# Filling the first buffer of a row-sum kernel with three loads in place of two

## The chip, the cores and the metric

The kernel runs on one core of a Trainium2 chip. The metric is device time in microseconds (us), the median of several runs. The engines that matter here are SyncE (SP), which issues all transfers; VectorE (DVE) and ScalarE (ACT), which add; and the core's 16 DMA engines, which move the data.

## The reference

```python
def setup_inputs():
    batch, seq, dim = 32, 512, 1024
    return {"x": np.random.randn(batch, seq, dim).astype(np.float32)}

def reference(x):
    return np.sum(x, axis=-1).astype(np.float32)
```

The input holds 16,384 rows of 1,024 float32 numbers, 67.1 MB in all. Each row is summed to one number, so the output is 64 KB. Every number is read once and added once.

## The kernel before, in words

The rows are spread over the 128 partitions of on-chip memory, 128 rows each. They are cut into three blocks of 32, 48 and 48 rows per partition (`BLOCKS`, line 10). Within a block, a partition's rows lie behind one another in memory, so that a partition's share of a load is one contiguous run.

Three buffers `xt0` to `xt2` of 16 rows per partition (64 KB per partition, 8.389 MB in all) are filled in turn. Lines 80 to 87 list the groups: seven of 16 rows. The last 16 rows come in smaller pieces: 9, 4 and 2 rows into the buffer that is then due (`CUTS`, lines 97 and 98), and the very last row in two parts of 544 and 480 columns into `tail` (lines 99 to 101).

Lines 92 to 95 write down the loads of the seven groups. Each group is one load, except the first, which is split in two: row 0 of each partition, which counts on the semaphore `first`, and rows 1 to 15, which count on `slot0`. A landed load adds 16 to its semaphore.

DVE waits for `first` (line 106) and then, for each group, for the group's slot (line 109). It then sums the whole group by one reduce over 16 rows (`rows_dve`, line 56). The first group's reduce thus starts when both loads have landed; no instruction uses row 0 alone. In the last group ACT takes 7 of the 16 rows (`rows_act`, line 67), and it takes a part of the pieces behind it. DVE sums the last rows by adding two halves (`pairs_dve`, line 74).

SP issues the loads in the order of the list (lines 135 to 138). From the fourth group on it first waits until DVE has summed what lay in the buffer. After the loads come three early stores of results, and then the last store (line 147).

All of this lies behind an opening barrier of the engines. Lines 174 to 182 take the first `EARLY` loads out of the body and put them ahead of SP's drain in the entry block, so that SP issues them before the barrier. `EARLY` is 2 here: both loads of the first group.

Of the kernel before, what the change touches and what calls it, by code (L numbers as in the profile page):

```python
# [11 lines left out]
BUFS = 3  # L12
ACT_ROWS = 7
CUT = 544
CUTS = (0, 9, 13, 15)
EARLY = 2


def row_sums(nc, x: bass.AP, out: bass.AP):
    P = nc.NUM_PARTITIONS  # L20
    x_flat = x.flatten_outer_dims()
    R, D = x_flat.shape
# [4 lines left out]
    xs, outs = [], []  # L27
# [6 lines left out]
    def sbuf(name, n):  # L34
        return nc.alloc_sbuf_tensor(name, [P, n], F32)

    xt = [sbuf(f"xt{i}", G * D) for i in range(BUFS)]
# [9 lines left out]
    sems = {n: nc.alloc_semaphore(n) for n in names}  # L47
    slots = [sems[f"slot{i}"] for i in range(BUFS)]
# [32 lines left out]
    for k, n in enumerate(BLOCKS):  # L81
        c = 0
        end = n - G if k == len(BLOCKS) - 1 else n
        while c < end:
            m = min(G, end - c)
# [4 lines left out]
    freed = {}  # L90
    loads = []
    for b, (k, c, m) in enumerate(groups):
        parts = [(0, m, slots[b % BUFS])] if b else [(0, 1, sems["first"]), (1, m, slots[0])]
        for i, j, s in parts:
            loads.append((b, xt[b % BUFS][:, i * D : j * D], xs[k][:, (c + i) * D : (c + j) * D], s))
    last = xt[n_bufs % BUFS]
    for k, (i, j) in enumerate(zip(CUTS, CUTS[1:])):
        loads.append((n_bufs, last[:, i * D : j * D], x_z[:, (z0 + i) * D : (z0 + j) * D], sems[f"piece{k}"]))
# [4 lines left out]

    nc.vector.memset(tail[:, CUT + 15 : CUT + 16], 0.0).then_inc(vec, 1)  # L104
    count["vec"] += 1
    nc.vector.wait_ge(sems["first"], 16)
    for b, (k, c, m) in enumerate(groups):
        a = ACT_ROWS if b == n_bufs - 1 else 0
        nc.vector.wait_ge(slots[b % BUFS], 16 * (b // BUFS + 1))
# [7 lines left out]
    for k in range(2):  # L117
        i, j = CUTS[k], CUTS[k + 1]
# [36 lines left out]
def kernel(tc: tile.TileContext, x: bass.AP, out: bass.AP):  # L155
    tc.close()
    tc.compile()  # L157
    nc = tc.nc
    row_sums(nc, x, out)

    sp = mybir.EngineType.SP
    fn = nc.m.functions[0]
    entry, body = None, None
    for blk in fn.blocks:
        ops = [i for i in blk.instructions if i.engine == sp]
        if entry is None:
            entry = blk
        elif any(i.opcode == "DMACopy" for i in ops):  # L170
            body = blk
            break
    code = list(body.instructions)
    loads = [i for i in code if i.engine == sp and i.opcode == "DMACopy"][:EARLY]
    for load in loads:
        assert not load.sync_info.on_wait
        code.remove(load)
    body.instructions = code
    code = list(entry.instructions)
    at = next(k for k, i in enumerate(code) if i.engine == sp and i.opcode == "Drain")  # L180
    code[at:at] = loads
    entry.instructions = code
# [29 lines left out]
```

## Time and profile before

| what | value |
|---|---|
| median of 3 runs | 160.51 us (160.5 to 160.61) |
| the profiled execution's own time | 160.68 us |
| span of that execution, first to last instruction | 159.3 us |
| DVE busy | 121.4 us (76%) |
| ACT busy | 17.2 us (11%) |
| read from HBM | 67.11 MB, 422 GB/s over the span |
| first load (512 KB), issue to landing | 3.5 us |
| second load (7680 KB), issue to landing | 21.3 us |

Times inside an execution count from the start of its span, which here is SP's first issue. The span is shorter than the execution's time by what lies around it, 1.38 us here. In the tables of stretches a DMA packet's bytes and time are booked to the stretch in which it starts; where packets last longer than a stretch, a share of DMA can exceed 1. Besides the groups and stretches, the trace has a record of every DMA packet: its start, its duration and its size. A packet is one partition's contiguous run of one load.

### The profile page before, as it was taken

To read this page: it belongs to the slowest core of one execution; us is meant where nothing else is said; L and a number is where in the kernel's file an instruction comes from. 1 tells how busy PE (TensorE), PEld (TensorE's weight loads), DVE (VectorE), ACT (ScalarE), POOL (GpSimd) and SP (SyncE) were. 2 spreads that over 40 slices of the span, in tenths; PEclk is the share of its full clock that TensorE was granted. 3 is DMA by queue.
4 is the path that set the end of the run, shared out by engine and by line. 5 is a ranking of instruction groups with operands and counts; after the bars stand their busy time and mean duration, and the time that the engine had idled before them with its cause. 6 is when DMAs were issued, how large, how long until landed. Compare 5 with 4: busy or idle time off the path is not lost.

```text
span 159.3 us, 109 instructions
## 1 busy us (share of the span) xinstructions
DVE 121.4 (76%) x16; ACT 17.2 (11%) x31; POOL 0.2 (0%) x4
## 2 busy tenths in 40 slices
DVE  0000059998699968999599994999949999499785
ACT  3000000000000000000000000000000000394694
POOL 0000000000000000000000000000000000000000
DMA  9988996996996999979969969969969989699994
GB/s 378 494 386 355 494 526 263 526 510 280 526 494 296 526 395 395 526 329 461 526 280 510 526 263 526 510 280 526 494 296 526 428 362 526 296 444 444 391 409 138
DMA packets 2448, 67.18 MB, mean 422 GB/s; under 512 B 784, under 2 KB 912, under 8 KB 1168
## 3 DMA queue, kind: packets, MB, share of 16 engines
q1 hardware_dynamic: 2448, 67.18, 98.1%
HBM read 67.11 MB, written 0.07 MB: 422 GB/s over the span
## 4 chain that ended last, share of the span: by engine, by line
DMA 75%; DVE 22%; SPq 1%; issue 0%
DMA xt<-in_x_dram 50%; DMA tail<-in_x_dram 25%; DVE res L56 22%; SPq L138 1%; DVE pairs L74 0%; DVE res L74 0%
## 5 line engine op out<-in xcount | busy, mean ns | idle before, releaser
L56 DVE TENSOR_REDUCE res<-xt 128x16 f32<-128x16384 f32 (+3 forms) x9 | 119.8, 13309 | 34.1 <-DMA xt<-in_x_dram 34.1
L67 ACT ACTIVATE xt<-xt 128x1024 f32<-128x1024 f32 x15 | 15.6, 1042 | 138.2 <-DMA xt<-in_x_dram 138.2
L67 ACT ACTIVATION_READ_ACCUMULATOR xt<-xt 128x1 f32 x15 | 2.8, 186 | 0.0
L104 DVE MEMSET tail<- 128x1 f32 x1 | 0.1, 59 | 2.0 <-PEq L157 2.0
L67 ACT ACT_TABLE_LOAD x1 | 1.3, 1283 | 1.9 <-PEq L157 1.9
L74 DVE CUSTOM_DVE_ANT_0 pairs<-tail 128x272 f32<-128x272 f32 (+1 forms) x2 | 0.9, 427 | 0.2 <-DMA tail<-in_x_dram 0.2
L74 DVE CUSTOM_DVE_ANT_0 pairs<-xt 128x512 f32<-128x512 f32 x1 | 0.7, 692 | 0.2 <-DMA xt<-in_x_dram 0.2
L74 DVE DVE_READ_ACCUMULATOR2_ANT res<- 128x1 f32 x2 | 0.2, 82 | 0.0
L196 POOL MEMSET const-bfloat16-1.0<- 128x1 bf16 x1 | 0.1, 102 | 0.0
L196 POOL MEMSET const-uint8-127<- 128x1 uint8 x1 | 0.1, 102 | 0.0
L196 POOL MEMSET const-float32-1.0<- 128x1 f32 x1 | 0.1, 99 | 0.0
L196 POOL MEMSET const-float32-0.0<- 128x1 f32 x1 | 0.1, 98 | 0.2 <-issue 0.2
L74 DVE DVE_READ_ACCUMULATOR2_ANT tail<- 128x1 f32 x1 | 0.1, 83 | 0.0
## 6 DMA issues: line engine op xcount, KB each, us to landing
xt<-in_x_dram SPq DMA_DIRECT2D x1, 7680.0 KB, 21.3
xt<-in_x_dram SPq DMA_DIRECT2D x1, 4608.0 KB, 32.4
xt<-in_x_dram SPq DMA_DIRECT2D x1, 2048.0 KB, 36.9
xt<-in_x_dram SPq DMA_DIRECT2D x1, 1024.0 KB, 38.9
xt<-in_x_dram SPq DMA_DIRECT2D x1, 512.0 KB, 3.5
tail<-in_x_dram SPq DMA_DIRECT2D x1, 272.0 KB, 39.1
tail<-in_x_dram SPq DMA_DIRECT2D x1, 240.0 KB, 39.2
xt<-in_x_dram SPq DMA_DIRECT2D x6, 40.8
```

The lines of the kernel that those rows point to most:

```text
L56: nc.vector.tensor_reduce(out=res[:, c : c + n], in_=t[:, j * D : (j + n) * D].rearrange("p (j d) -> p j d", d=D), axis=X, op=ADD,).then_i ...
L67: nc.scalar.activation(out=v, in_=v, func=COPY, accum_out=res[:, c + i : c + i + 1]).then_inc(act, 1)
L74: nc.vector.tensor_tensor_reduce(out=pairs[:, 0 : h - a], in0=t[:, a:h], in1=t[:, h:b], scale=1.0, scalar=0.0, op0=ADD, op1=ADD, accum_out ...
L104: nc.vector.memset(tail[:, CUT + 15 : CUT + 16], 0.0).then_inc(vec, 1)
L138: nc.sync.dma_start(out=dst, in_=src).then_inc(s, 16)
L196: nc = _bacc.Bacc("TRN2", target_bir_lowering=False, num_devices=1)
```

## The change

The first group is loaded by three loads: columns 0 to 511 of row 0, then the next 1,024 columns (the second half of row 0 and the first half of row 1), then the other 14.5 rows. The first two count on `first`, for which DVE now waits until 32; the third counts on `slot0`. `EARLY` becomes 3, so that all three are issued ahead of the barrier. The loads of the other groups are the same; their bounds are now written in columns.

```diff
-EARLY = 2
+EARLY = 3
+LEADS = (0, 512, 1536)
...
     for b, (k, c, m) in enumerate(groups):
-        parts = [(0, m, slots[b % BUFS])] if b else [(0, 1, sems["first"]), (1, m, slots[0])]
+        parts = [(0, m * D, slots[b % BUFS])]
+        if b == 0:
+            parts = [(i, j, sems["first"]) for i, j in zip(LEADS, LEADS[1:])] + [(LEADS[-1], m * D, slots[0])]
         for i, j, s in parts:
-            loads.append((b, xt[b % BUFS][:, i * D : j * D], xs[k][:, (c + i) * D : (c + j) * D], s))
+            loads.append((b, xt[b % BUFS][:, i:j], xs[k][:, c * D + i : c * D + j], s))
...
-    nc.vector.wait_ge(sems["first"], 16)
+    nc.vector.wait_ge(sems["first"], 32)
```

## The prediction

> **What bounds the kernel now.** I read the page from the top: the busy row of DMA, the share of the one queue, the chain of work that ended last.
>
> ```profile
> span 159.3 us, 109 instructions
> ...
> DMA  9988996996996999979969969969969989699994
> ...
> q1 hardware_dynamic: 2448, 67.18, 98.1%
> ...
> DMA 75%; DVE 22%; SPq 1%; issue 0%
> ```
>
> The reader is to see that the packets fill 98.1% of sixteen DMA engines' span. The chain's 22% of DVE is no second bound, as the groups and the waits show: DVE is released by a landing before every one of its reduces.
>
> ```profile
> L56 DVE TENSOR_REDUCE res<-xt 128x16 f32<-128x16384 f32 x6 | 103.3, 17220 | 30.4 <-DMA xt<-in_x_dram 30.4
> ...
> L56 DVE TENSOR_REDUCE res<-xt 128x4 f32<-128x4096 f32 x1 | 4.4, 4420 | 1.2 <-DMA xt<-in_x_dram 1.2
> ...
> L56 DVE TENSOR_REDUCE res<-xt 128x2 f32<-128x2048 f32 x1 | 2.3, 2285 | 0.5 <-DMA xt<-in_x_dram 0.5
> ```
>
> The timeline of DVE gives the pace: reduces of a full buffer start at 21.83, 41.10, 60.47, 79.82, 99.16 and 118.52 us, every 19.35 us or so, while one takes 17.22. A buffer is 8.389 MB, so the stream runs at 8.389 MB / 19.35 us = 434 GB/s. DVE waits 0.2 us for the last row pair and 0.2 us for the last tail piece too. Every wait on the way is ended by a landing, so **a shift of the whole DMA stream goes through to the end one for one**, in both directions.
>
> The change touches only the start of that stream. So the view that matters is the table of stretches at the start:
>
> ```profile
> core 0: us, DVE busy (x) ACT busy (x) POOL busy (x), PEclk, DMA share, GB/s
> 0.00:1.00 1.00, 0.00 (x0) 0.00 (x0) 0.20 (x4) 1.00 0.00 0
> 1.00:1.50 0.50, 0.00 (x0) 0.00 (x0) 0.00 (x0) 1.00 1.19 262
> 1.50:2.00 0.50, 0.02 (x1) 0.09 (x1) 0.00 (x0) 1.00 0.86 279
> ...
> 6.00:20.00 14.00, 0.00 (x0) 0.00 (x0) 0.00 (x0) 1.00 0.97 421
> ```
>
> Nothing moves in the first microsecond: the first load is issued at 0.00 and its first packet starts at 1.00 us. In the second microsecond the engines are occupied (a packet is booked where it starts, hence shares over 1) but move 262 and 279 GB/s instead of 434. That is a loss of about 0.38 us (1 - 270/434). The records of single DMA packets in the trace say where: the first load is 128 packets of 4,096 B, eight on each engine. The sixteen first ones start between 1.00 and 1.28 us. 89 of the 128 take under 170 ns (159 is typical) and 39 take up to 740, all of these started before 2.4 us. Per engine they sum to 1.65 us; eight at 157 ns, the usual pitch, would be 1.26. So **the start costs 0.40 us**, and the packets of the second load (61,440 B, typically 2,267 ns) another 0.11 us over that norm; two that started before 3 us exceed it by 268 and 327 ns. No engine stands idle between the two loads: added up, 15 to 16.5 engines are busy in every tenth of a microsecond from 1.2 us on.
>
> **The change part by part.** The same bytes come in the same order; one 4,096 B packet per partition becomes two, 2,048 and 4,096 B, and the long one shrinks from 61,440 to 59,392 B.
>
> *One more load.* 128 more packets and 16 more semaphore writes, so 8 and 1 on each engine. What a cut costs, from other packets of the trace: 8,192 B takes 309 ns and two of 4,096 B take 318, so 9 ns; 1,920 and 2,176 B together, again 4,096 B, take 79 + 88 = 167 against 159, so 8 ns. Eight cuts at 8.5 ns are 68 ns; a semaphore write is 9 ns. That makes **+0.08 us**.
>
> *Its issue.* SP's first two issues take 373 and 424 ns, at 0.00 and 0.42 us; a third, from about 0.9 us, takes some 0.43 (issues in a row take 437 to 462). While later loads were issued, at 58.35, 77.71 and 97.07 us, packets then in flight took about 15 ns longer. I put down **+0.01 us**.
>
> *What is moved.* The third load goes in ahead of SP's drain, so the opening barrier comes 0.45 us later, at about 2.35 instead of 1.9. Behind it stand SP's next issue (the load of buffer 1, at 1.91 now), ScalarE's table load and DVE's memset. The engines reach buffer 1 at 20.7 us, ACT's first row comes at 137.9, the zero is used at 157.4: all are covered by 17 us or more, and I put nothing down. If the cover were gone it would be 0.45 us. SP's later issues wait for DVE (112.3 us in five waits), so nothing is late there. POOL issues no load.
>
> *The wait.* DVE's first wait asks for 32 instead of 16: two loads landed rather than one. The first lands 3.5 us after issue now; the two will have landed by about 4 to 5 us. Behind it DVE has only the wait for the rest of the buffer, which ended at 21.8 us. It costs nothing, up to 17 us of delay.
>
> *Is the next load ready?* This trace doesn't show a first load so short. Each engine has eight packets of 2,048 B, about 80 ns each (1,920 B take 79 and 2,176 take 88): 0.65 us. An engine that loses nothing starts at 1.00 and would be through at 1.65. The second load is issued 0.42 us behind the first. Lags from issue to first packet with idle engines are 1.00 us (first load), 0.84 us (first store, 156.16 to 157.00) and 0.93 us (second store, 156.55 to 157.48). So its packets are due at 1.26 to 1.42 us, 0.2 us ahead of need. The third is due at about 1.9, and the second ends at 2.9 or later. I put down nothing; a lag over 1.22 us would show as idle engines.
>
> *The slow start.* What it becomes with shorter packets isn't in this trace, and I bound it from both sides. If slowness belongs to the first microsecond, whatever is asked for, it stays: 0. If it belongs to bytes in the first round of packets, half as many bytes could take as little as half of it, or all of 0.51 us might go. If it belongs to packets (39 of 128 slow), there are sixteen short ones per engine where there were eight, and another 0.40 us is lost. By time of start the mean is 327 ns up to 1.3 us, 243 to 1.6, 196 to 2.0, 166 to 2.4 and 159 after: it fades with time, while packet size is the same throughout. That is nearest to the first reading, so I take 0 and keep -0.51 and +0.40.
>
> **A rule against the change.** The last two loads, of 272 and 240 KB, run from full engines at 88 and 79 ns a packet (2,176 B / 88 ns x 16 = 395 GB/s): size alone hardly hurts a load that has others around it. The Trainium skill, page "DMA: Bandwidth & Descriptors", section "Bandwidth", tells authors to batch to 1 MiB or more, and its measured table has 64 KB in 0.95 us and 1 MB in 6.15 us. A line through these leaves about 0.6 us that every load would pay, an estimate from that page; by it the added load would make the kernel 0.6 us slower, while by the rows above it is 0.08. The page's figures are for loads issued from GpSimd, and no load here is.
>
> **The sum.** 0.08 + 0.01 + 0 + 0 = +0.09 us. Against the profiled execution (160.68 us: a span of 159.3 and 1.38 around it) that gives 160.77. That execution is 0.17 above the median of the runs shown, 160.51, so on the median I forecast **160.6 us**. A measurement of this kernel can tell about 0.2%, or 0.32 us, from no change, so the forecast is no change that can be told.
>
> **Rivals.**
>
> *Slower: the engines run dry or stumble more often at the start.* The place is 1.0 to 3 us. If the slow packets come per packet, the price is 0.40 us on top of 0.09: 161.0. If the second load is ready later than 1.22 us after its issue, each 0.1 us of it costs 0.1; this decides against me from a lag of about 1.45 us (0.32 - 0.09 = 0.23 over). For it: the first load's lag of 1.00 us was the longest of the three, and shorter packets meet the slow microsecond in greater number. Against it: the slow ones fade with time, and a lag of 1.45 us is half as long again as any seen.
>
> *Faster: short first packets take the slow start away.* The end is set by the engine that came last out of the start: last data packets end from about 156.4 to 156.96 us. If half of the 0.51 us goes, that is -0.26 + 0.09 = -0.17 and can't be told; if all goes, -0.51 + 0.09 = -0.42, which is 160.1; engines that end more evenly would add to it. For it: up to 2 us the engines move 270 of 434 GB/s, so there is something to win. Against it: the first byte isn't sooner, since the issue, not its size, sets that.
>
> *The change does nothing to the stream.* The order of SP's instructions has three loads ahead of the branch, of 512, 1024 and 14,848 columns, so it does what it says; this rival is left with the added packets alone and lies inside the forecast.
>
> **How the numbers follow.** Forecast, with what stays within 0.32 us of it: 0.47. Slower: 0.27. Faster: 0.26. The range reaches from 160.15 (all but the last of the slow start gone) to 161.0 (slow packets doubled), which leaves out about 2 in 10. The forecast's own range is 160.3 to 160.8. Chances: faster by over 0.2% 0.26, within 0.47, slower 0.27.
>
> **What would show it.** Right: a first packet at 1.00 us, no stretch under 15 busy engines after 1.2 us, about 270 GB/s in the second microsecond, the first full reduce at 21.9 us, then the same 19.35 us pace and the same 0.2 us waits at the end. A first reduce at 22.2 or later with the same pace is the slower rival; at 21.5 or before, the faster one. Wrong at the root: a pace other than 19.35 us, or a change of the end that the first reduce doesn't show; then the start isn't where the time went.

## The result, and the profile after

Five runs of the changed kernel have a median of 162.54 us (162.28 to 163.12), five of the kernel before 160.58 (160.5 to 160.68). The ratio is 1.0122, with a 95% interval of 1.0106 to 1.0139. The change makes the kernel 1.96 us **slower**. The forecast was 160.6 us, no change that can be told, in a range up to 161.0; it was wrong.

The page of the profiled execution (162.45 us, a span of 161.1), the lines that answer to those of before:

```profile
span 161.1 us, 110 instructions
...
DMA  9899999989989999999999999999999989998992
...
q1 hardware_dynamic: 2592, 67.18, 97.5%
...
DMA 75%; DVE 22%; SPq 1%; issue 0%
...
L57 DVE TENSOR_REDUCE res<-xt 128x16 f32<-128x16384 f32 (+3 forms) x9 | 119.8, 13309 | 35.5 <-DMA xt<-in_x_dram 35.5
```

and the last of these lines before the change:

```profile
L56 DVE TENSOR_REDUCE res<-xt 128x16 f32<-128x16384 f32 (+3 forms) x9 | 119.8, 13309 | 34.1 <-DMA xt<-in_x_dram 34.1
```

There are 144 packets more (128 of data and 16 semaphore writes), the same bytes, and the same chain. DVE's reduces cost the same 119.8 us; they wait 35.5 us for landings, where it was 34.1. (That is 1.4 us and not 1.8, because DVE passes the barrier 0.47 us later and so begins to wait later.) DVE's own timeline says when the time was lost; first the first two reduces of before, then those of after:

```profile
21.83 17.22 DVE L56 TENSOR_REDUCE res<-xt 128x16 f32<-128x16384 f32 x1 [19.79 <-DMA xt<-in_x_dram]
41.10 17.22 DVE L56 TENSOR_REDUCE res<-xt 128x16 f32<-128x16384 f32 x1 [2.06 <-DMA xt<-in_x_dram]
```

```profile
23.66 17.22 DVE L57 TENSOR_REDUCE res<-xt 128x16 f32<-128x16384 f32 x1 [21.15 <-DMA xt<-in_x_dram]
42.94 17.22 DVE L57 TENSOR_REDUCE res<-xt 128x16 f32<-128x16384 f32 x1 [2.05 <-DMA xt<-in_x_dram]
62.28 17.22 DVE L57 TENSOR_REDUCE res<-xt 128x16 f32<-128x16384 f32 x1 [2.13 <-DMA xt<-in_x_dram]
...
139.69 9.75 DVE L57 TENSOR_REDUCE res<-xt 128x9 f32<-128x9216 f32 x1 [2.12 <-DMA xt<-in_x_dram]
```

The first reduce starts at 23.66 instead of 21.83 us, 1.83 later. The pace behind it is the old one (19.28 and 19.34 us), the nine-row piece is 1.82 us later, and the span 1.8 longer. So all of the loss lies ahead of 23.66 us, and nothing of it is won back. The table of stretches of that start:

```profile
core 0: us, DVE busy (x) ACT busy (x) POOL busy (x), PEclk, DMA share, GB/s
...
1.00:1.50 0.50, 0.00 (x0) 0.00 (x0) 0.00 (x0) 1.00 0.92 197
1.50:2.00 0.50, 0.00 (x0) 0.00 (x0) 0.00 (x0) 1.00 0.94 332
...
4.00:4.50 0.50, 0.00 (x0) 0.00 (x0) 0.00 (x0) 1.00 0.42 119
```

The first microsecond of the stream moves (197 + 332) / 2 = 264 GB/s; it was 270. The leads, as I call the short loads ahead of the long one, are as good as before. What is new comes after them. A stretch's DMA share books a packet where it starts, so I add up the records of single packets, as the prediction did, into the number of engines with a packet in work:

```
engines busy, mean of each 0.5 us from 1.0 us on
before  12.8 15.9 16.0 16.3 16.0 16.0 16.0 16.0 16.0 16.0
after   10.8 16.4 15.4 16.4 14.8 12.0 13.3 15.1 16.0 16.0
```

From 3 to 5 us up to a quarter of the engines have nothing to do. The third load was issued at 0.89 us. Its first packets, one on each engine, start between 3.17 and 4.73 us, though the second load's last packet had started at 3.49. And the packets that do run are long: 2,192 ns is the length of an undisturbed packet of 59,392 B, and nineteen of the first thirty take 160 to 1,210 ns more, all started before 6.7 us. Taking size / 27.13 B per ns + 8 ns as the norm, the long packets exceed it by 0.87 us per engine (0.06 before), the idle time is 0.32 us per engine (0.01 before), and the short packets exceed theirs by 0.29 (0.38 before).

Added up with 0.08 us for the packets that were cut, this is 0.31 + 0.81 - 0.09 + 0.08 = 1.11 us per engine, and the mean landing of the first buffer on an engine is in fact 1.17 us later (21.31 to 22.48). The rest is unevenness: the engines land between 21.90 and 23.57 us, a spread of 1.67 where it was 0.72, and DVE waits for the last one. The last one is 1.84 us later.

SP's rows hold one more trace of it. In the view of its issues (count; shortest, median, longest in ns):

```profile
L141 SPq DMA_DIRECT2D xt<-in_x_dram x12: 327/350/1368, 0.0 to 119.1; - x12
```

The 1,368 ns are SP's fifth issue, at 2.76 us; the longest before took 462. SP itself was held up, from 2.76 to 4.13 us, while the third load's first packets were starting.

### The profile page after: what moved, and what is told of

Same layout as the page of the kernel before. It is cut to its first block, busy times and chain, and to the rows that moved or that the text cites. A ratio compares the mean times of both kernels' runs of the same rounds, so it can differ in the third digit from the quotient of the medians.

```text
span 161.1 us, 110 instructions
## 1 busy us (share of the span) xinstructions
DVE 121.4 (75%) x16; ACT 17.2 (11%) x31; POOL 0.2 (0%) x4
## 4 chain that ended last, share of the span: by engine, by line
DMA 75%; DVE 22%; SPq 1%; issue 0%
DMA xt<-in_x_dram 50%; DMA tail<-in_x_dram 24%; DVE res L57 21%; SPq L141 1%; DVE pairs L75 0%; DVE res L75 0%
## 5 line engine op out<-in xcount | busy, mean ns | idle before, releaser
L57 DVE TENSOR_REDUCE res<-xt 128x16 f32<-128x16384 f32 (+3 forms) x9 | 119.8, 13309 | 35.5 <-DMA xt<-in_x_dram 35.5
```

The lines of the kernel that those rows point to most:

```text
L57: nc.vector.tensor_reduce(out=res[:, c : c + n], in_=t[:, j * D : (j + n) * D].rearrange("p (j d) -> p j d", d=D), axis=X, op=ADD,).then_i ...
```

## Experiments

Unless a diff says otherwise, each kernel is the changed one with `LEADS` and `EARLY` as given (the wait on `first` asks for 16 per lead). "Ratio" is to the kernel before, run on the same chip.

| kernel | median us | ratio, 95% interval |
|---|---|---|
| three loads, third behind the barrier | 161.74 | 1.0069 [1.0047, 1.0092] |
| two loads, three issues ahead of the barrier | 160.56 | 1.0000 [0.9990, 1.0011] |
| one lead of 1,536 columns | 160.72 | 1.0006 [0.9994, 1.0019] |
| next loads held back | 162.65 | 1.0121 [1.0093, 1.0149] |
| long second load | 160.97 | 1.0022 [1.0002, 1.0042] |
| one lead of 512 columns | 160.96 | 1.0025 [1.0009, 1.0040] |
| 1,024 and 1,024 columns | 161.15 | 1.0037 [1.0018, 1.0057] |
| long load first | 160.90 | 1.0016 [1.0005, 1.0027] |
| mid-stream, 2 rows left, 8,192 B packets | 160.82 | 1.0013 [0.9997, 1.0029] |
| mid-stream, 2 rows left, 2,048 B packets | 160.89 | 1.0015 [1.0004, 1.0026] |
| leads by partition | 162.60 | 1.0117 [1.0094, 1.0141] |
| 1,024 and 1,024, third behind the barrier | 162.23 | 1.0094 [1.0067, 1.0120] |
| restart with two loads | 162.85 | 1.0150 [1.0122, 1.0177] |
| restart with three loads | 164.77 | 1.0243 [1.0200, 1.0285] |
| third load on ACT's queue | 161.02 | 1.0024 [1.0015, 1.0034] |

### First round: is it the third load, the packets, or the barrier?

My theory was late supply: a load issued while packets flow is not there when it is needed. The rivals: short packets or odd offsets (A), three issues ahead of the barrier (B), the issues that follow (C).

*Third load behind the barrier* (its expectation, then the result):

```diff
-EARLY = 3
+EARLY = 2
```

> The changed kernel, but only the first two loads are issued ahead of the barrier; the third goes out at about 1.9 us instead of 0.89. Theory (late supply: a load that is issued while packets already flow reaches the engines several us after its issue, so the third load is not there when the second ends at about 3.3 us): as slow as the changed kernel or up to 1 us slower, 162.5 to 163.6 us. Rival A (2,048 B packets or the offset of 6,144 B slow the reading, whenever the load is issued): 162.5 us. Rival B (three issues ahead of the barrier are what hurts): back to 160.6 us.

161.74 us: not the old time, but below the 162.5 to 163.6 that the theory allowed, and faster than the changed kernel. Rival B falls as the whole cause, since the loss is still 1.1 us with two early issues. But the theory in its plain form, a fixed delay behind the issue, is hit too: issued a whole microsecond later, the third load's first packets start at 3.11 to 4.03 us, earlier at the end than the 4.73 of the changed kernel. All sixteen of them run 350 to 1,010 ns long.

*Three issues ahead of the barrier, two loads for the buffer:*

```diff
-LEADS = (0, 512, 1536)
+LEADS = (0, 1024)
```

> One lead of 1,024 columns as in the kernel before, but three loads ahead of the barrier: the third is the load of the second buffer, which the engines reach only at about 20 us. Theory (late supply): the third load has 20 us to arrive, so 160.6 us, like before. Rival A (short packets or offset): 160.6 us. Rival B (three issues ahead of the barrier hurt): 162 us or more, with engines idle between 3 and 4.5 us.

160.56 us, the old time. Three early issues cost nothing when the third load is the next buffer's, needed at 20 us. Rival B is out.

*One lead of 1,536 columns:*

```diff
-EARLY = 3
-LEADS = (0, 512, 1536)
+EARLY = 2
+LEADS = (0, 1536)
```

> Two loads for the first buffer, of 1,536 columns and of the other 14.5 rows: the long packets are 59,392 B at an offset of 6,144 B as in the changed kernel, but there is no third load. Theory (late supply): the second load, issued at 0.42 us, has until about 2.9 us, so 160.6 us. Rival A in the form that the offset or the packet size hurts: about 162 us, with packets of 59,392 B far over 2,192 ns.

160.72 us, within the uncertainty the old time. Its long load is the same 128 packets of 59,392 B at the same offset as in the changed kernel, first needed at the same time (3.18 to 3.71 us). Fifteen of its first sixteen take 2,192 or 2,193 ns, the other 2,245. So neither size nor offset nor the moment, some 3 us into the kernel, makes those packets long. What differs is that the load came third, and that it was issued 0.47 us nearer to its need (2.3 us ahead, against 2.8 here). The first reduce of this kernel:

```profile
21.69 17.22 DVE L57 TENSOR_REDUCE res<-xt 128x16 f32<-128x16384 f32 x1 [19.65 <-DMA xt<-in_x_dram]
```

It starts 0.14 us earlier than in the kernel before and 1.97 earlier than in the changed one.

*Next loads held back:*

```diff
+        if n == EARLY:
+            nc.sync.wait_ge(sems["first"], 32)
```

> The changed kernel, but SP issues the loads of the second and third buffer only when both leads have landed, at about 4 us. Theory (late supply of the third load itself): no gain, about 162.5 us. Rival C (the issues of the next two loads, at 2.4 and 2.8 us, crowd out the third one): 160.6 to 161.2 us, engines busy without a gap.

162.65 us, as slow as the changed kernel, with the issues of the next two loads moved to 4.01 and 4.39 us. The loads that follow are not what delays the third. Rival C is out.

### Second round: how long is the third load's delay?

*Long second load:*

```diff
-LEADS = (0, 512, 1536)
+LEADS = (0, 512, 8192)
```

> The changed kernel with a longer second load: the three loads have 512, 7,680 and 8,192 columns, all issued ahead of the barrier. The engines need the third one only at about 11 us (1.0 + 0.65 for the first + 8 x 1.14 for the second), 10 us after its issue. Theory (a third load that is needed within some 3 us of its issue is not there yet): no loss, 160.6 to 160.8 us, engines busy without a gap. Rival A (the 2,048 B packets of the first load, or the cut inside a row, slow what follows): 161.5 us or more. Rival B (three loads for one buffer ahead of the barrier cost as such): 161.5 us or more.

160.97 us: the loss of 1.96 shrinks to 0.35. Three loads are nearly free when the second lasts until 11 us. The rest is more than I expected; in this profile the third load's packets are undisturbed and it is the second load's first packets that run long, 0.25 us per engine. But the profiled execution is the fastest of the ten (160.53, of 160.53 to 161.83), so where the 0.35 us of the median come from is not shown.

*One lead of 512 columns, two loads:*

```diff
-EARLY = 3
-LEADS = (0, 512, 1536)
+EARLY = 2
+LEADS = (0, 512)
```

> Two loads for the first buffer, of 512 columns and of the other 15.5 rows, both ahead of the barrier. The engines are through with the first at 1.7 to 2.0 us, some 1.3 us after the issue of the second. Theory: in the changed kernel the second load was there in time under the same conditions, so no loss or a small one, 160.6 to 160.9 us. Rival A (packets of 2,048 B slow what follows): 161.5 us or more.

160.96 us, just above what the theory allowed. Needed 1.5 us after its issue, the second load too is met while it is still arriving: in the profiled execution, one of the slower ones (161.56 us), its first packets run long by 0.33 us on the mean engine and by 0.88 on the worst. SP's fourth issue takes 839 ns there.

*1,024 and 1,024 columns:*

```diff
-LEADS = (0, 512, 1536)
+LEADS = (0, 1024, 2048)
```

> Three loads for the first buffer, of 1,024, 1,024 and 14,336 columns, all ahead of the barrier: no packet of 2,048 B and no cut inside a row, but the third load is needed at about 3.9 us, 3.0 us after its issue (in the changed kernel 2.3 us after). Theory: part of the loss stays, 161.1 to 162.2 us, with some engines idle around 4 to 5 us. Rival A (short packets or the cut inside a row): 160.6 us.

161.15 us: with 3.0 us from issue to need in place of 2.3, 0.53 of the 1.96 us stay, without a short packet or a cut inside a row. In the profiled execution, again one of the slower ones (161.78 us), one engine's first long packet starts last of all, at 4.51 us, and runs 1.12 us over; that engine lands the buffer at 22.87 us, the mean one at 21.67. One late engine is enough.

*Long load first*, the same three loads in another order:

```diff
+                parts = [(LEADS[-1], m * D, slots[0])] + [ ...the two leads... ]
```

> The same three loads as in the changed kernel, with the same packets, issued ahead of the barrier in another order: the 14.5 rows first, then 512, then 1,024 columns. Each engine has 17 us of work from the first load alone. Theory: no load is needed soon after its issue, so 160.5 to 160.8 us. Rival A (sizes and offsets of these packets): 162 us or more. Rival B (three issues ahead of the barrier): 162 us or more.

160.90 us, 0.1 above what the theory allowed. The very packets of the changed kernel, without its loss; only the slow start is 0.3 us dearer, because the first sixteen packets are the long ones and each runs 0.4 to 1.0 us over. Rival A is out: it is the order.

### Third round: the middle of the stream, and a count of packets

Was this a delay that every load has, and nobody sees because later loads are issued 20 us ahead? Two kernels issue the second buffer's load only when all but two rows of the first have landed:

```diff
+            parts = [(0, D, sems["first"]), (D, TAILS[0], sems["mid"])]
+            parts += ...the last two rows, in one load or in four, at TAILS...
...
+        if n == held:
+            nc.sync.wait_ge(sems["mid"], 16)
```

> The kernel before, with the first buffer in three loads of 1, 13 and 2 rows, and SP issuing the loads of the second and third buffer only when the 13 rows have landed, at about 19 us. The engines then have the 2 rows left, eight packets of 8,192 B or some 2.5 us, less what the faster ones are ahead. This measures in the middle of the stream how late a load may be issued. If a load is ready about 1 us after its issue, as the first one and the stores were: no gap, 160.6 to 160.9 us. If a load under traffic always takes 2.3 to 3.8 us, as the third one of the changed kernel did: engines idle at 20 to 22 us and 161.3 to 162.6 us.

> As the kernel with the 2 rows left, but these come as four loads of 512 columns, 32 packets of 2,048 B on each engine, or some 2.7 us. Theory P (a load arrives late when it is issued while the engines work through short packets): the next buffer's load comes late though there is as much work left, 161.2 to 163 us with engines idle at 20 to 23 us. Theory S (only the start of the kernel is slow) and theory T (it is the time from issue to need alone): no more than 0.3 us above the variant with 8,192 B packets.

160.82 and 160.89 us: no loss beyond that of the cuts. In the first of the two the load is issued at 19.22 us and its first packets start between 20.77 and 21.30, each right behind the engine's last short one; no engine runs dry. So the first of two loads issued in mid-stream is there 1.5 us later, in time, and the second kernel shows that short packets ahead of it do no harm. A general delay is out, and so is my theory P, that short packets in the way make the next load late.

*Leads by partition*, four loads with half as many, longer packets ahead of the long one:

```diff
-EARLY = 3
+EARLY = 4
...
+            for p, q in ((0, 32), (32, 96), (96, 128)):
+                loads.append((0, xt[0][p:q, 0 : 2 * D], xs[k][p:q, 0 : 2 * D], sems["first"]))
```

> The first two rows are cut by partitions: three leads of 32, 64 and 32 partitions with packets of 8,192 B, two, four and two on each engine, then one load of the other 14 rows; four loads ahead of the barrier. The fourth is issued at about 1.35 us and needed at 3.6 to 3.9, as soon after its issue as the third in the changed kernel, but with 8 longer packets ahead of it in place of 16 shorter ones. Theory P (short packets in the way make the next load late): 160.6 to 161.1 us. Theory T (time from issue to need alone, or the number of loads): 162 us or more.

162.60 us, against theory P. But the test isn't clean: cut this way the leads themselves run 1.21 us per engine over the norm, more than in any other kernel, so part of the loss is their own.

*1,024 and 1,024 columns, third load behind the barrier:*

```diff
-EARLY = 3
-LEADS = (0, 512, 1536)
+EARLY = 2
+LEADS = (0, 1024, 2048)
```

> The three loads of 1,024, 1,024 and 14,336 columns again, but the third is issued behind the barrier, at 1.9 us instead of 0.9, and needed at 3.9. If the time from issue to need alone decides (theory T): clearly slower than the same loads all ahead of the barrier, which took 161.15 us, so 161.6 to 162.5. If an issue close behind two others, into engines that just begin on short packets, is what makes it late (theory P): the same or faster, 160.7 to 161.2 us.

162.23 us, 1.1 us slower than with all three ahead of the barrier. Here a later issue hurts, as time from issue to need would have it; with 512 and 1,024 columns it had helped by 0.8 us (162.54 to 161.74). Against theory P again, and a sign that the delay isn't one number.

### Fourth round: a burst into idle engines, or the beginning of the program?

Two kernels load the first buffer as the kernel before does, let the engines come to a standstill, and then load the second buffer by two or by three loads:

```diff
+            parts = [(i, j, sems["mid"]) for i, j in zip(AGAIN, AGAIN[1:])] + [(AGAIN[-1], m * D, slots[1])]
...
+        if n == held:
+            nc.sync.wait_ge(slots[0], 16)
```

`AGAIN` is (0, 1024) in the one and (0, 512, 1536) in the other.

> The kernel before, with a standstill made on purpose: SP issues nothing beyond the first buffer until that buffer has landed (about 21.7 us), and the second buffer is then loaded by two loads, of 1,024 and 15,360 columns. The engines run dry at 21.0 to 21.4, the first new packet comes about 1 us after the issue, and the ramp costs some 0.4 us: 162.2 to 162.9 us. It is the control for its twin with three loads.

> The same standstill, but the second buffer is then loaded by three loads, of 512, 1,024 and 14,848 columns, as the changed kernel does at its start. If three loads in a row into engines that stand still make the third one late, wherever this happens (theory R): 1 to 2.2 us above the twin with two loads, 163.4 to 165 us. If it is the beginning of the program alone that makes it late (theory S): within 0.3 us of the twin.

162.85 and 164.77 us. The twins differ by 1.92 us, as the kernel before and the changed one do (1.96), 22 us behind the beginning. (The four runs of the second twin reach from 164.0 to 165.48 us, and the profiled one is the longest, so that its reduce below is 2.69 us later.) The second buffer's reduce, with two loads and then with three:

```profile
43.31 17.22 DVE L58 TENSOR_REDUCE res<-xt 128x16 f32<-128x16384 f32 x1 [4.42 <-DMA xt<-in_x_dram]
```

```profile
46.00 17.22 DVE L58 TENSOR_REDUCE res<-xt 128x16 f32<-128x16384 f32 x1 [7.10 <-DMA xt<-in_x_dram]
```

Both had their first reduce at 21.68 us. And the stretches behind the restart, of the twin with two loads and of that with three:

```profile
24.00:25.00 1.00, 1.00 (x1) 0.00 (x0) 0.00 (x0) 1.00 2.56 1081
25.00:26.00 1.00, 1.00 (x1) 0.00 (x0) 0.00 (x0) 1.00 0.00 0
26.00:27.00 1.00, 1.00 (x1) 0.00 (x0) 0.00 (x0) 1.00 2.27 983
```

```profile
24.00:25.00 1.00, 1.00 (x1) 0.00 (x0) 0.00 (x0) 1.00 2.30 862
25.00:26.00 1.00, 1.00 (x1) 0.00 (x0) 0.00 (x0) 1.00 1.16 356
26.00:27.00 1.00, 1.00 (x1) 0.00 (x0) 0.00 (x0) 1.00 0.22 59
```

With two loads, all sixteen engines take up their first long packet by 25 us and, 2.3 us later, their second: nothing starts in the stretch between. With three, the first long packets straggle in up to 26.76 us, the excess of the long load is 0.95 us per engine against 0.07, and the idle time 0.28 against 0.03. The picture of the changed kernel's start is drawn again. It is not the beginning of the program; it is three loads issued in a row into engines that stand still, the third of them needed at once. Nor is it the time alone that the long load has: with two loads it is issued at 21.98 us and its first packet starts at 24.11, 2.1 us later; with three, at 22.45 and 24.71, 2.3 us later. The second load of a row is in time after 2.1 us, the third isn't after 2.3.

*Third load on ACT's queue:*

```diff
+    nc.scalar.dma_start(out=loads[2][1], in_=loads[2][2]).then_inc(loads[2][3], 16)
...all loads behind it on nc.scalar too; SP issues the two leads; ACT's first one also moved ahead of the barrier
```

> The changed kernel's loads, but SP issues only the two leads; the 14.5 rows and all loads behind them are issued by ACT, the 14.5 rows ahead of the barrier at about 0.1 us. The long packets then wait in a second queue from about 1 us on. If the third load of the changed kernel is late because it goes through one queue behind two others (theory Q): 160.5 to 161.0 us. If the third load is late on any path (theory S in its widest form): 162 us or more.

161.02 us, 1.57 of the 1.96 us gone, two hundredths above what theory Q allowed. But more than the path has changed. Each engine takes up its first long packet between 1.72 and 2.81 us, ahead of any packet of the second lead, and the long packets exceed the norm by only 0.11 us per engine. The second lead, on the other queue, then goes through one packet at a time between the long ones, from 4.35 to 21.41 us, and it is its landing at 23.92 that the first reduce waits for:

```profile
23.94 17.22 DVE L57 TENSOR_REDUCE res<-xt 128x16 f32<-128x16384 f32 x1 [21.90 <-DMA xt<-in_x_dram]
```

That is later than in the changed kernel, and yet the kernel is faster, because the engines are busy without a gap. So the same three loads need not cost 1.96 us, which agrees with theory Q. Whether a long load that really comes behind both leads would be in time on a second queue isn't shown: here the engines reach it ahead of the second lead, and it is issued 0.77 us earlier. No run separates path, order and earlier issue.

## Why the prediction was wrong

**The bound and the way to the end** held. The whole shift of the stream, 1.83 us at the first reduce, arrives at the end as 1.8 us, and the waits of the full reduces behind it are as long as before (2.05 to 2.14 us).

**One more load**, +0.08 us, and **its issue**, +0.01 us: not contradicted. The two mid-stream kernels, which add one and four loads that nothing waits for at once, are 0.15 and 0.22 us above the kernel before. The 15 ns by which packets in flight were said to take longer during an issue are 8 to 13 on average in the records; the term stays at 0.01.

**What is moved** and **the wait** cost nothing, as predicted: with three issues ahead of the barrier and two loads for the buffer the time is 160.56 us, and in the changed kernel both leads have landed by 3.99 us, long before the rest of the buffer at 23.57.

**"Is the next load ready?"** is the step that failed. It said that the third load "is due at about 1.9, and the second ends at 2.9 or later", and put down nothing. The due time was built from lags of 0.84 to 1.00 us, each of a load or store that the engines were waiting for, first or second in its row. The third load of a row isn't like these: issued at 0.89 us, it reached the engines from 3.17 to 4.73 us, though they were through with the second load by 3.65, and its packets ran up to 1.2 us over their normal length until 6.7 us. The trace of before couldn't show this. Its third load is issued at 1.9 us and needed at 20.7, and any delay up to 18 us is invisible there. A lag measured on the first load was used as if it were a property of every load, which the text didn't bound from above.

**The slow start** was bounded at -0.51 and +0.40 us and taken as 0. Of the leads this was about right: their packets exceed the norm by 0.29 us per engine where it was 0.38. The loss isn't in them.

**The rival** "slower: the engines run dry or stumble more often at the start" had the signs right, idle engines and a first reduce at 22.2 us or later, but the place too early (1 to 3 us; it is 3 to 6.7). It looked at the wrong load, the second, which came in time. Its 161.0 came from slow packets alone, and for a late load it gave a rate but no amount. Its prices were also means over the engines, while the buffer is complete only when the slowest has landed: 0.67 us of the 1.83 are that unevenness (1.84 for the last engine less 1.17 for the mean).

**The rule of the Trainium skill** ("DMA: Bandwidth & Descriptors", section "Bandwidth") to load 1 MiB or more at a time pointed the right way, but not at what happened. The estimate from its table, 0.6 us for any added load, would hold for the kernel with the long second load and the one with the long load first as well; these lose 0.35 and 0.28 us. The price depends on how soon the load behind is needed.

**What stays open** is the inside of it: why the third load of a burst arrives late and piecemeal, and whether it is its place in SP's queue alone that does it. A fixed time from issue to arrival doesn't fit (issued a microsecond later, the third load came earlier in one pair of kernels and cost 1.1 us more in the other), and a count of packets ahead doesn't either (sixteen on each engine in four kernels, which lose 0.53, 1.11, 1.56 and 1.96 us). That SP's issues stall for 1,368, 839 and 1,082 ns in three of the slow kernels, but not in others as slow, is seen and not explained.

## What to carry to other kernels

Where a stream of loads starts, or restarts, into engines that stand still, put at most one short load in front of a long one. Here one lead of 1,024 or 1,536 columns cost nothing, one of 512 columns 0.34 us; a second short lead made the long load third in the queue and cost 1.96 us, over 20 times the 0.08 us estimated for the added packets. Read a load's lag from a row in which something waited for that very load, in the same place of the queue; where the trace has no such row, the lag's upper end is the whole cover. And look at the spread of the engines' landings, not at their mean: the slowest of sixteen sets the time.

## What the runs showed of the hardware

A burst of three loads into idle engines delivers the third late. Its first packets start 2.3 to 3.8 us after its issue, the last of them 1.1 us after the engines were through with the load ahead, and run up to 1.2 us over. The first load starts 1.0 us after its issue, and the first of two loads in mid-stream was there within 1.5 us. The loss repeats at a standstill in the middle of the kernel (1.92 us) as at its beginning (1.96).

The engines hardly even out. In the changed kernel they land the first buffer 1.67 us apart and the very last load still 1.65 us apart, from 157.57 to 159.22 us; in the kernel before it is 0.72 and 0.60, with one lead of 512 columns 1.26 and 1.02. A spread that arises at the start is for the most part kept through 135 us of streaming, and DVE waits for the last engine.
